# Four gate tiles of a hybrid layer as 2x2x2 block products with seven multiplications

## The chip, the cores and the metric

The kernel runs on one core of a Trainium2 chip. The core has a matrix engine (TensorE, PE in the profile, with its weight loads as PEld), a vector engine (VectorE, DVE), a scalar engine (ScalarE, ACT), a general one (GpSimd, POOL), and queues that issue transfers from memory; SP is the one that issues most. Each engine takes its instructions in the order of the program and waits at semaphores for the others. The metric is the device time of one execution in microseconds (us); the median of three runs is taken.

## The reference

One layer on x of 512 tokens by 1024 channels, in fp32, with 8 attention heads, a memory of 256 tokens and an FFN with 2816 hidden channels:

```python
h = rms_norm(x, norm_mix)
q_a, k_a, v_a, u_b, gate_b, gate_c, g_a, g_b = split(h @ w_in)   # 6 x 512, then 2 x 1024 columns
o_a = stick_breaking_attention(q_a, k_a, v_a)
y_b = gate_b * causal_depthwise_conv(gate_c * u_b, conv_w)
merged = sigmoid(g_a) * (o_a @ w_branch_a) + sigmoid(g_b) * (y_b @ w_branch_b)
x = x + merged @ w_mix_out
x = x + memory_cross_attention(rms_norm(x), rms_norm(mem), w_mem_q, w_mem_kv, w_mem_o)
gate, up = split(rms_norm(x, norm_ffn) @ w_ffn_in)
x = x + (silu(gate) * up) @ w_ffn_out
return rms_norm(x, norm_final)
```

The change is in g_a and g_b, the two gates of 1024 channels each, and in what lies beside them.

## The kernel before

Activations are kept transposed, as tiles of 128 channels by 512 tokens. To keep fp32's precision, each operand is split into a high part (rounded, on ACT) and a remainder (on DVE), and each product is made of three matmuls, high by high, high by remainder, remainder by high (`mm3`, lines 159 to 161). A weight tile of 128 x 1024 (512 KB) is loaded by SP into a buffer `wr`, of which there are four, cast on ACT to `wh` (line 154) and its remainder `wl` made on DVE (line 155).

A wide product of one column tile with 8 tiles of x is 24 matmuls of 512 columns. The layer has also the other kind: two column tiles, two halves of the tokens and two tiles of the inner dimension form a 2x2x2 block product, which is made with seven multiplications in place of eight (`product`, line 710; the products go to PSUM tiles z, v and y). It needs sums of blocks of x (`forms_of`, from two tiles xe and xo: c and d are the sums; high parts xf, xoh, xch, xdh, remainders xol, xcl, xdl) and of the weights (`ffn_raw` on DVE or POOL; `ffn_form` makes their high and low parts), and sums of the products behind it (`reads`, `second`). The seven products are 12 matmuls of 256 columns each, at a time. Memory queries and FFN are made so before; the gates are not.

Stages: projections and the attention, one step after another (`scores`: ACT makes Abs, Exp and Ln of z as e, DVE adds, POOL masks; `parts`: e is cast and split into l; `weights`: matmuls of l with negtri, line 437, then Exp as a, masked by POOL and split on DVE into ah and al; `values`). TensorE's order there is written out; projections, convolution and the first gate tiles fill its time between the steps, and weight loads go along with them. The orders of ACT, DVE, POOL and SP in this stage come out of a scheduler. Then a loop over the 8 column tiles of the gates: per tile two gate products (`pr`, 24 matmuls each; DVE multiplies by the tokens' norm factor; ACT takes the sigmoid), the two branch products (`br`, 12 matmuls each), two multiplications by DVE (line 583), their sum (line 584) and its split (`mh`, `ml`). Then the output projection, tile by tile (`r`), which adds x (`residual`, line 630) from tiles that SP loads into xpool, eight buffers, and makes the forms for the memory queries.

From the memory queries on, the orders of TensorE, ACT and DVE are written out. The SP queue takes its loads in one order, and a load whose buffer isn't free holds those behind it.

## Time and profile before

| | |
|---|---|
| median of 3 runs | 852.45 us (852.08 to 853.06) |
| the profiled execution | 852.67 us, of which 851.0 are the span |
| TensorE busy | 843.5 us (99%) |
| VectorE busy | 644.3 us (76%) |
| ScalarE busy | 460.9 us (54%) |
| GpSimd busy | 77.2 us (9%) |
| gates, tiles 4 to 7 | 236.60 to 301.90 us |
| output projection | 301.90 to 345.50 us |

The page gives each engine's busy time and share, the clock that the throttle granted TensorE, and the chain that ended last. Since matmuls follow one another with hardly a gap, the list of what TensorE waited for is the view to look at when something is added, and the timeline, where it is queried by engine and stretch, shows how near each chain came. Rows of the timeline read: start, length, engine, line, operation, outputs<-inputs, shape, count; idle time of the engine just before and what ended it in brackets.

### The profile page before, as it was taken

How to read it: one execution, taken by the hardware profiler on the slowest of the kernel's cores; microseconds unless marked ns; L12 is line 12 of the kernel's file. 1: busy time of each engine (PE TensorE's matmuls, PEld its weight loads, DVE VectorE, ACT ScalarE, POOL GpSimd, SP SyncE). 2: the span in 40 equal slices, each digit the busy share in tenths (PEclk: the TensorE clock that was granted, in tenths of full speed). 3: DMA queues.
4: the chain of work that ended last, by engine and by line, in shares of the span. 5: the costliest groups of instructions: out<-in, count | busy, mean ns of one | idle time of the engine just before them, and what ended most of it. 6: DMA issues, size and time to landing. Idle time of an engine off the chain costs nothing.

```text
span 851.0 us, 13532 instructions
## 1 busy us (share of the span) xinstructions
PE 843.5 (99%) x5200; PEld 757.9 (89%) x5200; DVE 644.3 (76%) x1106; ACT 460.9 (54%) x822; POOL 77.2 (9%) x101
## 2 busy tenths in 40 slices
PE   9999999999999999999999999999999999999997
PEld 7878787888888888999988889999999999888997
DVE  8769889987444467878765889888888778876864
ACT  7566767665333245665654666555445556552444
POOL 1011112211000001000000110111111110010002
PEclk9999999999999999999999999999999999999999
DMA  8332332318333334655331427777677775362312
GB/s 298 130 118 76 99 101 73 101 51 271 112 99 99 99 99 113 158 188 189 124 109 65 137 60 199 182 187 178 175 189 186 191 188 170 128 149 68 97 38 100
DMA packets 47217, 114.71 MB, mean 135 GB/s; under 512 B 4912, under 2 KB 9008, under 8 KB 47152
## 3 DMA queue, kind: packets, MB, share of 16 engines
q1 hardware_dynamic: 38704, 97.82, 35.1%
q0 software_dynamic: 8160, 15.73, 11.7%
q8 instruction: 41, 0.67, 0.3%
q14 instruction: 24, 0.20, 0.1%
q10 hardware_dynamic: 288, 0.29, 0.1%
HBM read 110.65 MB, written 2.10 MB: 132 GB/s over the span
## 4 chain that ended last, share of the span: by engine, by line
PE 99%; DVE 0%; POOL 0%; issue 0%; DVEq 0%; ACT 0%; POOLq 0%
PE z L710 20%; PE y L710 10%; PE pr L159 8%; PE pr L161 8%; PE pr L160 8%; PE v L710 5%; PE r L159 3%; PE r L161 3%; PE r L160 3%; PE f L160 3%; PE f L161 3%; PE f L159 3%; PE v L265 3%; PE br L159 2%; PE br L161 2%; PE br L160 2%
## 5 line engine op out<-in xcount | busy, mean ns | idle before, releaser
L154 ACT CAST wh<-wr 128x1024 fp32r<-128x1024 f32 x90 | 94.2, 1050 | 130.0 <-issue 48.1
L155 DVE TENSOR_TENSOR wl<-wr,wh 128x1024 fp32r<-128x1024 f32 x90 | 109.6, 1221 | 18.0 <-ACT wh L154 17.2
L159 PE MATMUL pr<-xgh,wh 128*128 128x512 f32 x288 | 112.6, 391 | 0.0
L160 PE MATMUL pr<-xgl,wh 128*128 128x512 f32 x288 | 112.3, 390 | 0.0
L161 PE MATMUL pr<-xgh,wl 128*128 128x512 f32 x288 | 112.2, 390 | 0.0
L710 PE MATMUL z<-xdh,wf 128*128 128x256 f32 x480 | 95.7, 283 | 0.0
L710 PEld LDWEIGHTS z<-xdh,wf 128*128 128x128 f32 x480 | 78.9, 192 | 0.0
L710 PE MATMUL z<-xdl,wf 128*128 128x256 f32 x240 | 67.9, 283 | 0.0
L733 ACT COPY sa<-z 128x256 f32<-128x256 f32 x52 | 19.4, 373 | 85.5 <-PE z L710 85.4
L161 PEld LDWEIGHTS pr<-xgh,wl 128*128 128x128 f32 x288 | 54.0, 188 | 11.4
L159 PEld LDWEIGHTS pr<-xgh,wh 128*128 128x128 f32 x288 | 54.1, 188 | 11.2 <-DVE rv L128 0.3
L160 PEld LDWEIGHTS pr<-xgl,wh 128*128 128x128 f32 x288 | 54.1, 188 | 10.9
L701 DVE TENSOR_TENSOR wf<-s,wf 128x512 fp32r<-128x512 f32 x60 | 41.3, 690 | 22.8 <-ACT wf L700 21.6
L667 POOL DMA_DIRECT2D ws<-in_w_ffn_in_dram x22 | 26.4, 1202 | 301.8 <-DMA ws<-in_w_ffn_in_dram 140.4
L700 ACT CAST wf<-ws 128x512 fp32r<-128x512 f32 x60 | 36.9, 618 | 24.9 <-PE r L160 10.0
L159 PE MATMUL f<-acth,wh 128*128 128x512 f32 (+1 forms) x144 | 49.3, 342 | 0.0
L160 PE MATMUL f<-actl,wh 128*128 128x512 f32 (+1 forms) x144 | 49.3, 342 | 0.0
L161 PE MATMUL f<-acth,wl 128*128 128x512 f32 (+1 forms) x144 | 49.1, 342 | 0.0
L692 DVE TENSOR_TENSOR wf<-wg,wf 128x1024 fp32r<-128x1024 f32 x30 | 36.7, 1224 | 16.0 <-ACT wf L691 15.9
L710 PE MATMUL y<-xch,wf 128*128 128x256 f32 x240 | 48.5, 283 | 0.0
L710 PE MATMUL v<-xoh,wf 128*128 128x256 f32 x240 | 48.5, 283 | 0.0
L710 PE MATMUL z<-xf,wf 128*128 128x256 f32 x360 | 48.4, 283 | 0.0
(295 smaller groups left out, 2296.0 us busy)
## 6 DMA issues: line engine op xcount, KB each, us to landing
wr<-in_w_in_dram SPq DMA_DIRECT2D x36, 512.0 KB, 3.5
ws<-in_w_ffn_in_dram SPq DMA_DIRECT2D x22, 512.0 KB, 3.9
ws<-in_w_ffn_in_dram POOLq DMA_DIRECT2D x22, 512.0 KB, 6.0
wg<-in_w_ffn_in_dram SPq DMA_DIRECT2D x22, 512.0 KB, 4.8
wr<-in_w_ffn_out_dram SPq DMA_DIRECT2D x14, 512.0 KB, 3.5
a<-in_w_ffn_in_dram SPq DMA_DIRECT2D x22, 256.0 KB, 4.9
wr<-in_w_branch_dram SPq DMA_DIRECT2D x8, 512.0 KB, 3.5
wr<-in_w_mix_out_dram SPq DMA_DIRECT2D x8, 512.0 KB, 3.4
```

What stands on the lines that cost most here:

```text
L154: after(nc.scalar.copy(h2, raw), lead[-1:])
L155: lows.append(nc.vector.tensor_tensor(out=l2, in0=raw, in1=f(h2), op=ALU.subtract))
L159: nc.tensor.matmul(ps, a[0], b[0], start=start, stop=False, **kw)
L160: nc.tensor.matmul(ps, a[0], b[1], start=False, stop=False, **kw)
L161: nc.tensor.matmul(ps, a[1], b[0], start=False, stop=stop, **kw)
L265: nc.tensor.matmul(vps[t], xg[k][a][:, sl], wv[k][b], start=k == 0 and (a, b) == (0, 0), stop=k == KD - 1 and a == 1)
L667: nc.gpsimd.dma_start(s13, a[:, 0:4:3, :], accum_op=ALU.add)
L692: nc.vector.tensor_tensor(out=lo, in0=pair, in1=f(hi), op=ALU.subtract)
L700: nc.scalar.copy(hi, raw)
L701: nc.vector.tensor_tensor(out=lo, in0=raw, in1=f(hi), op=ALU.subtract)
L710: nc.tensor.matmul(ps[:, :HS], a, b, start=i < 3 and k == 0 and j == 0, stop=k == KP - 1 and j == 2, skip_group_check=True)
L733: nc.scalar.copy((s[:, :HS], None, None, s[:, HS:], t[:, :HS], t[:, :HS])[i], z)
```

## The change

The gates of the last four column tiles (4 to 7) are made as 2x2x2 block products with seven multiplications: the two column tiles of a block are gate A's and gate B's of the same channels, and per tile there are 84 matmuls of 256 columns in place of 48 of 512. Their weights come as a new input in block order, and are loaded and summed like those of the FFN, four forms ahead (`GATE_AHEAD`). The sums of x that they need are made of x times the norm's gains: `pair_load` loads two tiles of x once more into a buffer `wr` in the loop over the first four tiles (on SP), `pair_forms` scales them on ACT (lines 774 to 776), makes the sums on DVE and splits them on both; the high parts and remainders of x itself are there from the attention's projections. The order of TensorE, ACT and DVE in these four tiles is written out: product, sums of products (`gate_reads`, `gate_second`), next forms, and behind each tile's last product its branch products. The splits of the merged tiles are made later: tiles 0 to 3 during the last tile's products, 4 to 7 behind the last branch; until then the merged sums stay in xpool. The x of the residual, for which xpool's eight buffers served before, is now taken from the unit pool (`f(unit("x"))`), and the split parts of d (xdh, xdl) from xpool (`new=spare`).

```diff
+GATES = 4
+GM = QM + D // (2 * P)
+GATE_AHEAD = 4
...
-    def split(src, s, scale=None, cols=512):
-
-        hi, lo = unit(s + "h", cols), unit(s + "l", cols)
+    def split(src, s, scale=None, cols=512, new=unit):
+
+        hi, lo = new(s + "h", cols), new(s + "l", cols)
...
+    def spare(s, cols=512):
+        return xpool.tile([P, cols], F32R, tag="x", name=nm(s), padded_shape=[P, S])
...
-    merged = []
-    for m in range(KD):
-        sig = []
-        for j in range(2):
-            if (m, j) not in gates:
-                gate(m, j)
-            t = gates.pop((m, j))
-            sigmoid = nc.scalar.activation(t, t, AF.Sigmoid)
-            after(sigmoid, exps[-2:])
-            sig.append(t)
-        w = load_w(wbr_d[m])
-        for j, act in ((1, yb), (0, oT)):
-            ps = mmtile("br")
-            gemm(ps, w, act, 4 * j)
-            nc.vector.tensor_tensor(out=sig[j], in0=ps, in1=sig[j], op=ALU.mult)
-        nc.vector.tensor_tensor(out=sig[0], in0=sig[0], in1=sig[1], op=ALU.add)
-        merged.append(split(sig[0], "m"))
...
+        return c, d
+
+    def forms_of(xe, xo):
+
+        b11 = xe[:, :HS]
+        c, d = sums_of(xe, xo)
...
-        (oh, ol), (ch, cl), (dh, dl) = split(xo, "xo"), split(c, "xc"), split(d, "xd")
+        (oh, ol), (ch, cl), (dh, dl) = split(xo, "xo"), split(c, "xc"), split(d, "xd", new=spare)
+        return listed((u[:, :HS], u[:, HS:]), oh, ol, ch, cl, dh, dl)
+
+    def listed(first, oh, ol, ch, cl, dh, dl):
         a, b = slice(0, HS), slice(HS, S)
-        return [(u[:, a], u[:, b]), (oh[:, a], ol[:, a]), (ch[:, a], cl[:, a]),
-                (dh[:, a], dl[:, a]), (ch[:, b], cl[:, b]), (dh[:, b], dl[:, b]),
-                (oh[:, b], ol[:, b])]
+        return [first, (oh[:, a], ol[:, a]), (ch[:, a], cl[:, a]), (dh[:, a], dl[:, a]),
+                (ch[:, b], cl[:, b]), (dh[:, b], dl[:, b]), (oh[:, b], ol[:, b])]
...
-                xm = xpool.tile([P, S], F32, tag="x", name=nm("x"))
+                xm = f(unit("x"))
...
-        src = wfi_d[m] if m < NF else wfp_d[m - NF] if m < QM else wmq_d[m - QM]
+        src = (wfi_d[m] if m < NF else wfp_d[m - NF] if m < QM else wmq_d[m - QM] if m < GM
+               else wga_d[m - GM])
...
-            xh, xl = (x2f if m < NF else af if m < QM else x1f)[k][i]
+            xh, xl = (x2f if m < NF else af if m < QM else x1f if m < GM else x0f)[k][i]
...
+    merged, halves0, raw_m = [], [], []
+
+    def branch(m, sig, w):
+        for j, a in ((1, yb), (0, oT)):
+            ps = mmtile("br")
+            gemm(ps, w, a, 4 * j)
+            nc.vector.tensor_tensor(out=sig[j], in0=ps, in1=sig[j], op=ALU.mult)
+        t = f(spare("m"))
+        nc.vector.tensor_tensor(out=t, in0=sig[0], in1=sig[1], op=ALU.add)
+        raw_m.append(t)
+
+    def squash(t):
+        sigmoid = nc.scalar.activation(t, t, AF.Sigmoid)
+        after(sigmoid, exps[-2:])
+        return sigmoid
+
+    def pair_load(k2):
+        xp = wpool.tile([P, 2, S], F32, tag="wr", name=nm("xp"))
+        nc.sync.dma_start(xp, xT_d[2 * k2 * P:(2 * k2 + 2) * P, :].rearrange("(j p) t -> p j t",
+                                                                            p=P))
+        return xp
+
+    def pair_forms(k2, xp):
+        for j in range(2):
+            k = 2 * k2 + j
+            nc.scalar.activation(xp[:, j, :], xp[:, j, :], AF.Copy, scale=g_mix[:, k:k + 1])
+        c, d = sums_of(xp[:, 0, :], xp[:, 1, :])
+        (eh, el), (oh, ol) = xg[2 * k2:2 * k2 + 2]
+        return listed((eh[:, :HS], el[:, :HS]), oh, ol, *split(c, "xc"), *split(d, "xd"))
+
+    x0f = []
+    for m in range(KD - GATES):
+        sig = []
+        for j in range(2):
+            if (m, j) not in gates:
+                gate(m, j)
+            sig.append(gates.pop((m, j)))
+            squash(sig[j])
+        if m < KD // 2:
+            xp = pair_load(m)
+        branch(m, sig, load_w(wbr_d[m]))
+        if m < KD // 2:
+            x0f.append(pair_forms(m, xp))
+
+    def gate_reads(m, i):
+        b = banks[m]
+        z, g, t = b["z"][:, :HS], b["g"] if "g" in b else None, b["t"]
+        lo, hi = slice(0, HS), slice(HS, S)
+        if i == 0:
+            b["z0"] = tmp("fg")
+            nc.scalar.copy(b["z0"][:, lo], z)
+        elif i == 1:
+            b["g"] = g = b["z0"]
+            nc.vector.tensor_tensor(out=g[:, lo], in0=b["v"][:, :HS], in1=g[:, lo], op=ALU.add)
+        elif i == 3:
+            nc.scalar.copy(g[:, hi], z)
+        elif i == 4:
+            nc.scalar.copy(t[:, hi], z)
+        elif i == 5:
+            for u, half in ((z, lo), (t[:, hi], hi)):
+                nc.vector.scalar_tensor_tensor(out=t[:, half], in0=u, scalar=-1.0,
+                                               in1=r0b[:, half], op0=ALU.mult, op1=ALU.mult)
+            squash(t)
+        elif i == 6:
+            nc.vector.tensor_tensor(out=g[:, hi], in0=b["y"][:, :HS], in1=g[:, hi], op=ALU.add)
+            nc.vector.tensor_tensor(out=g, in0=g, in1=r0b, op=ALU.mult)
+            b["sigmoid"] = squash(g)
+
+    def gate_second(m):
+        b = banks[m]
+        t = b["t"][:, HS:]
+        nc.vector.tensor_tensor(out=t, in0=b["y"][:, :HS], in1=t, op=ALU.add)
+
+    gs = order(GM, GATES)
+    for n in range(GATE_AHEAD + SUM_AHEAD):
+        ffn_raw(*gs[n], nc.gpsimd)
+    for n in range(GATE_AHEAD):
+        ffn_form(*gs[n])
+    with tc.manual_schedule(engines={mybir.EngineType.PE, mybir.EngineType.Activation,
+                                     mybir.EngineType.DVE}):
+        wb, last_m = {}, GM + GATES - 1
+        for n, (m, i) in enumerate(gs):
+            product(bank_of(m, i), m, i)
+            if i == 1 and m > GM:
+                gate_second(m - 1)
+            elif (m, i) == (last_m, 5):
+                gate_second(m)
+            gate_reads(m, i)
+            if n + GATE_AHEAD < len(gs):
+                ffn_form(*gs[n + GATE_AHEAD])
+            if n + GATE_AHEAD + SUM_AHEAD < len(gs):
+                ffn_raw(*gs[n + GATE_AHEAD + SUM_AHEAD])
+            if i == 3:
+                wb[m] = load_w(wbr_d[KD - GATES + m - GM])
+            if i == 6:
+                b = banks.pop(m)
+                branch(KD - GATES + m - GM, (b["g"], b["t"]), wb[m])
+                sigmoid = b["sigmoid"]
+            if m == last_m and i in (1, 2, 3, 4):
+                merged.append(split(raw_m[len(merged)], "m"))
+        while len(merged) < KD:
+            merged.append(split(raw_m[len(merged)], "m"))
...
+    def by_block(w, n=None):
+
+        w = w.reshape(-1, 2, P, NB, 2, P) if n is None else (
+            w.reshape(-1, 2, P, 2, n, P).transpose(0, 1, 2, 4, 3, 5))
+        return w.transpose(3, 2, 4, 1, 0, 5).reshape(-1, P, 2048)
...
+        "w_gates": by_block(w_in[0][:, O_A:O_A + 2 * D], KD)[KD - GATES:],
```

The orders of the engines change in three places that are looked at below. In the ACT order of a late attention step (e is the step's z through Abs, Exp and Ln; a the Exp of the step before), before:

```order
L154 CAST wh_1880<-wr_1878 128x1024
L400 ACTIVATE e_1648<-z_1644 128x256
L445 ACTIVATE a_1659<-z_1511 128x512
L445 ACTIVATE a_1661<-z_1512 128x512
L401 ACTIVATE e_1648<-e_1648 128x256
L402 ACTIVATE e_1648<-e_1648 128x256
L410 COPY carry_397<-z_1644 1x256
L373 CAST l_1673<-e_1648 128x256
L154 CAST wh_1997<-wr_1995 128x1024
```

and after (line numbers are 3 higher there):

```order
L157 CAST wh_1880<-wr_1878 128x1024
L776 ACTIVATE xp_2106<-xp_2106,gcol 128x512 x2
L403 ACTIVATE e_1648<-z_1644 128x256
L448 ACTIVATE a_1659<-z_1511 128x512
L448 ACTIVATE a_1661<-z_1512 128x512
L404 ACTIVATE e_1648<-e_1648 128x256
L405 ACTIVATE e_1648<-e_1648 128x256
L413 COPY carry_397<-z_1644 1x256
L376 CAST l_1673<-e_1648 128x256
L157 CAST wh_1997<-wr_1995 128x1024
```

The two scalings of the first x pair, xp, now stand between a weight cast and the Abs. At the end of the gates, DVE before (g is a gate, br a branch product, x the residual):

```order
L583 TENSOR_TENSOR g_2753<-br_2762,g_2753 128x512
L583 TENSOR_TENSOR g_2719<-br_2776,g_2719 128x512
L584 TENSOR_TENSOR g_2719<-g_2719,g_2753 128x512
L155 TENSOR_TENSOR wl_2935<-wr_2932,wh_2934 128x1024
L174 TENSOR_TENSOR ml_2792<-g_2719,mh_2791 128x512
L630 TENSOR_TENSOR x_2827<-r_2802,x_2827 128x512
```

and after, where fg and sb are a tile's two gates (A and B) and y the PSUM tile of its last product:

```order
L757 TENSOR_TENSOR sb_2696<-br_3018,sb_2696 128x512
L757 TENSOR_TENSOR fg_2709<-br_3032,fg_2709 128x512
L759 TENSOR_TENSOR m_3046<-fg_2709,sb_2696 128x512
L822 TENSOR_TENSOR sb_2862<-y_2920,sb_2862 128x256
L811 SCALAR_TENSOR_TENSOR sb_2862<-z_2861,r0b_338 128x256
L811 SCALAR_TENSOR_TENSOR sb_2862<-sb_2862,r0b_338 128x256
L158 TENSOR_TENSOR wl_3167<-wr_3164,wh_3166 128x1024
L815 TENSOR_TENSOR fg_2875<-y_2920,fg_2875 128x256
L158 TENSOR_TENSOR wl_3227<-wr_3224,wh_3226 128x1024
L816 TENSOR_TENSOR fg_2875<-fg_2875,r0b_338 128x512
L757 TENSOR_TENSOR sb_2862<-br_3079,sb_2862 128x512
L757 TENSOR_TENSOR fg_2875<-br_3093,fg_2875 128x512
```

The first reading of the last tile's y (line 822) stands behind the branch multiplications and the sum of the tile before; weight remainders stand among them, and the splits `ml` of tiles 4 to 7 come after the last sum. In the forms of the last pair of x tiles ahead of the memory queries, DVE before:

```order
L603 TENSOR_TENSOR xf_3172<-xr_3125,xf_3172 128x256
L174 TENSOR_TENSOR xol_3176<-xr_3164,xoh_3175 128x512
L174 TENSOR_TENSOR xcl_3180<-c_3166,xch_3179 128x512
L174 TENSOR_TENSOR xdl_3184<-c_3167,xdh_3183 128x512
L735 TENSOR_TENSOR qa_3238<-v_3237,sa_3226 128x256
```

and after:

```order
L596 TENSOR_TENSOR xf_3503<-xr_3456,xf_3503 128x256
L177 TENSOR_TENSOR xol_3507<-xr_3495,xoh_3506 128x512
L177 TENSOR_TENSOR xdl_3515<-c_3498,xdh_3514 128x512
L177 TENSOR_TENSOR xcl_3511<-c_3497,xch_3510 128x512
L732 TENSOR_TENSOR qa_3569<-v_3568,sa_3557 128x256
```

The remainder of d stands ahead of that of c; the high parts on ACT have changed places in the same way, and so have both ahead of the FFN.

13 lines of the change are left out of this document (6 added, 7 removed).

## The prediction

> **What bounds the kernel now.** I read the page first, then the waits of TensorE, then windows and stretches of the timeline where the change puts something. Two parts of the page:
>
> ```profile
> span 851.0 us, 13532 instructions
> PE 843.5 (99%) x5200; PEld 757.9 (89%) x5200; DVE 644.3 (76%) x1106; ACT 460.9 (54%) x822; POOL 77.2 (9%) x101
> PEclk9999999999999999999999999999999999999999
> PE 99%; DVE 0%; POOL 0%; issue 0%; DVEq 0%; ACT 0%; POOLq 0%
> ```
>
> And the whole answer on what TensorE (PE) waited for:
>
> ```profile
> engine line waited for: us in total, times, longest us
> PE warm L224 <- DVE neg L91: 1.6, 1, 1.6
> ```
>
> So TensorE is the path from end to end, at full granted clock: work taken off it shortens the run by as much, and every new wait of it lengthens the run by as much. The profiled execution took 852.67 us, of which 851.0 is the span; the median of the three runs is 852.45, 0.2 below. About 0.2%, 1.7 us, is what a measurement of this kernel can tell from no change: under 850.75 is faster, over 854.15 slower.
>
> **The gain.** Windows of the gate stage before (tiles 4 to 7) and of a stretch of the FFN that already consists of such products (length; busy time and instructions of PE, PEld, DVE, ACT, POOL; granted clock; share of the DMA engines; GB/s):
>
> ```profile
> 236.60:301.90 65.30, 65.30 (x290) 54.07 (x289) 30.59 (x36) 20.67 (x26) 0.00 (x0) 1.00 0.30 97
> 506.89:567.09 60.20, 60.20 (x503) 60.11 (x502) 54.09 (x96) 34.30 (x63) 7.22 (x6) 1.00 0.74 178
> ```
>
> Before, four tiles are 4 x 72 = 288 matmuls of 512 columns, 65.3 / 288 = 0.2267 us each. A 256-column one takes 60.2 / 503 = 0.120 us: more than half of 0.2267, with weight loading (PEld) busy for all of the window. Per tile 48 x 0.2267 = 10.88 us of gate matmuls become 7 x 12 x 0.120 = 10.08; 0.80 saved, four times: 3.2 us. The branch matmuls stay.
>
> [...]
>
> VectorE (DVE) has room: the FFN window needs 54.09 / 60.2 x 10.08 = 9.1 us of it per tile. A gate tile needs about as much, plus a branch's share (two multiplications and a sum of 0.69, a weight remainder of 1.22: 3.3), in 10.08 + 5.44 = 15.5 us. The sums, splits and scalings of x go into the attention, where nothing of them is on TensorE: their work is covered, and what counts is who waits behind them (waits 1 to 3).
>
> **Wait 1: x at the head of ScalarE (ACT).** In the order of ACT the two scalings of the first x pair stand in front of the Abs of a late attention step. Its chain before:
>
> ```profile
> wr<-in_w_branch_dram SPq DMA_DIRECT2D x2, 512.0 KB, 3.5
> 154.37 0.33 SPq L147 DMA_DIRECT2D wr<-in_w_branch_dram  x1
> 155.39 0.38 ACT L400 ACTIVATE e<-z 128x256 f32<-128x256 f32 x1
> 155.66 1.08 ACT L445 ACTIVATE a<-z 128x512 f32<-128x512 f32 x2
> 156.32 1.89 POOL L359 TENSOR_SCALAR_AFFINE_SELECT a<-a 128x128 f32<-128x128 f32 x2 [6.92 <-ACT a L445]
> 157.07 0.42 ACT L402 ACTIVATE e<-e 128x256 f32<-128x256 f32 x1
> 158.75 0.42 DVE L453 CAST ah<-a 128x512 fp32r<-128x512 f32 x1
> 159.75 0.42 DVE L403 SCALAR_TENSOR_TENSOR e<-z,e 128x256 f32<-128x256 f32 x1
> 160.21 0.36 ACT L410 COPY carry<-z 1x256 f32<-1x256 f32 x1 [2.71 <-DVE e L403]
> 160.24 1.13 POOL L359 TENSOR_SCALAR_AFFINE_SELECT e<-e 128x256 f32<-128x256 f32 x1 [2.04 <-DVE e L403]
> 161.41 0.41 ACT L373 CAST l<-e 128x256 fp32r<-128x256 f32 x1 [0.84 <-POOL e L359]
> 161.85 0.42 DVE L374 TENSOR_TENSOR l<-e,l 128x256 fp32r<-128x256 f32 x1 [0.74 <-ACT l L373]
> 162.61 0.40 PE L437 MATMUL z<-l,negtri 128*128 128x256 f32 x2
> 346.31 0.73 ACT L633 ACTIVATE xr<-x,gcol 128x512 f32<-128x512 f32 x1 [0.33 <-DVE x L630]
> 346.94 0.62 ACT L642 ACTIVATE sq<-x 128x512 f32<-128x512 f32 x1
> ```
>
> The x load takes the queue slot of the branch weight, which is issued at 154.37 and needs 3.5: it lands at 157.9. Two scalings follow, 0.63 from start to start (346.31 to 346.94), so the Abs starts at 159.2 in place of 155.39, 3.85 late. POOL's mask of a then starts at 160.2, its first half ends at 161.1, and DVE, which in its order takes ah and a convolution step (0.6) ahead of e, reaches e at 162.2 in place of 159.75: it had 2.26 in hand (157.49 to 159.75), and uses part of it. From there the distances stay: 162.7 POOL, 163.9 ACT, 164.3 DVE, which ends at 164.7; TensorE follows 0.25 later at 164.95 in place of 162.6. That is 2.3 us. All of TensorE is queued behind it, so nothing covers it. Ends: 1.5, if all of the 2.26 absorbs; 3.7, if none does. I take 2.3, since the DVE order gives that point.
>
> That a row of ACT holds what is written behind it is seen at 160.21: ACT stood 2.71 us for DVE and none of its later rows ran. [...]
>
> **Wait 2: the second x pair.** It stands on ACT before a weight cast and the next step's Abs; its second scaling and one weight cast stand ahead of the two casts l, and on DVE g and wl come ahead of the two remainders l:
>
> ```profile
> 176.52 0.93 ACT L373 CAST l<-e 128x384 fp32r<-128x384 f32 x2 [0.94 <-DVE e L424]
> 177.07 1.03 DVE L374 TENSOR_TENSOR l<-e,l 128x384 fp32r<-128x384 f32 x2 [0.30 <-ACT l L373]
> 178.01 0.69 DVE L311 TENSOR_TENSOR g<-pr,r0b 128x512 f32<-128x512 f32 x1
> 178.61 1.22 DVE L155 TENSOR_TENSOR wl<-wr,wh 128x1024 fp32r<-128x1024 f32 x1
> 180.56 0.97 PE L437 MATMUL z<-l,negtri 128*128 128x384 f32 x4
> ```
>
> Now ACT is free at 175.6 for the scaling (0.63) and the cast (1.04), so wl can't start before 177.3; if g comes where it did, at 178.0, wl ends at 179.8, the remainders (0.52 each) at 180.8, and TensorE goes on at 181.05 in place of 180.56: 0.5. Ends: 0, if g is ready earlier and wl follows the cast at once (remainders done at 179.7); 1.1, if g, wl, scaling and cast all add up (0.60 + 1.14 + 0.63 + 0.95 + 0.25 to TensorE, less the 2.46 between 178.10 and 180.56). I take 0.5, the value that the rows give.
>
> **Wait 3: end of attention.** The third x load goes ahead of branch weights, whose cast came just in time:
>
> ```profile
> 193.59 0.33 SPq L147 DMA_DIRECT2D wr<-in_w_branch_dram  x1
> 197.57 1.05 ACT L154 CAST wh<-wr 128x1024 fp32r<-128x1024 f32 x1 [1.59 <-PE pr L160]
> 201.43 0.69 DVE L583 TENSOR_TENSOR g<-br,g 128x512 f32<-128x512 f32 x1 [0.22 <-PE br L161]
> ```
>
> The cast begins 3.98 after the issue, and TensorE's first use of the sublayer's output follows within a few us. Before, that load had 256 KB pieces of x around it; now it has 512 KB of x just ahead on SP's queue, and ACT has two scalings to fit in. The cast may come from 0 to 1.0 later (a weight cast of 1.05 ahead of it at most); I take 0.3, nearer to the low end, because ACT stood idle 1.59 before it.
>
> **Wait 4: last two gate tiles.** The last tile's final product writes a PSUM tile that DVE must have read; that read stands behind both branch multiplications and the sum of the tile before. The same instructions before:
>
> ```profile
> 301.64 0.39 PE L161 MATMUL br<-oh,wl 128*128 128x512 f32 x1
> 302.07 0.69 DVE L583 TENSOR_TENSOR g<-br,g 128x512 f32<-128x512 f32 x1 [1.96 <-PE br L161]
> 302.79 0.69 DVE L584 TENSOR_TENSOR g<-g,g 128x512 f32<-128x512 f32 x1
> L743 DVE TENSOR_TENSOR sb<-y,sb 128x256 f32<-128x256 f32 x22 | 9.2, 418 | 0.0
> ```
>
> From the branch's last matmul (its slot ends at 301.87) to the multiplication 0.2, then 0.72, 0.61, 0.42, and 0.25 to TensorE: 2.2 us, of which one product (12 x 0.120 = 1.44) covers part: 0.75, taken as 0.7. Ends 0.4 and 1.2 (a weight remainder of 1.22 slipping in between, less what it hides). The merged splits 4 to 7 behind the last branch: the sum ends at 303.5, then four remainders and a wl at 0.6 and 1.14, so the one for tile 5 ends at 305.8 and TensorE wants it at 301.87 + 18 x 0.2267 = 305.95, less than 0.25 later: 0.1. The residual's x, loaded ahead before, is now issued on SP behind the last mix weight that waits for tile 3's remainder (about 305.6 by the row of DVE that it waits for):
>
> ```profile
> x<-in_xT_dram SPq DMA_DIRECT2D x8, 256.0 KB, 5.6
> ```
>
> It lands by 311.2, and the PSUM buffer that it holds up is wanted two blocks of 24 matmuls after the stage's start, at 301.9 + 10.9 = 312.8, less 0.7 for the addition: nothing, with 0.9 in hand. Ends of these: 0 and 0.3 for the splits; the x, if it comes a landing later, is part of the much slower rival.
>
> **Wait 5: the swap of two remainders.** In the forms of the last pair, at the start of the memory queries and again of the FFN, DVE now makes xdl before xcl. Both places before:
>
> ```profile
> 349.68 0.69 DVE L174 TENSOR_TENSOR xcl<-c,xch 128x512 fp32r<-128x512 f32 x1
> 350.42 0.39 PE L710 MATMUL y<-xcl,wf 128*128 128x256 f32 x1
> 505.65 0.68 DVE L174 TENSOR_TENSOR xcl<-c,xch 128x512 fp32r<-128x512 f32 x1
> 506.39 0.39 PE L710 MATMUL y<-xcl,wf 128*128 128x256 f32 x1
> ```
>
> TensorE takes xcl 0.05 after it is ready, so it is the wait already; 0.6 later (one remainder, start to start) costs 0.6 at each place, 1.2. The later xdl products want xdl only after that. Ends 0.6 (one place) and 1.4.
>
> **The sum.** -3.2 + 2.3 + 0.5 + 0.3 + 0.7 + 0.1 + 1.2 = +1.9: 854.6 against 852.67 of the profiled execution, and 854.4 against the median. With all low ends (1.5, 0, 0, 0.4, 0, 0.6) it is -0.7: 851.8; with all high ends (3.7, 1.1, 1.0, 1.2, 0.3, 1.4) it is +5.5: 858.0, both against the median.
>
> **The rivals.**
> - Faster: the attention absorbs the x loads, in that x lands sooner or DVE's 2.26 us in hand and later slack take all of it. With waits 1 to 3 gone, wait 4 at 0.4 and one of the two swaps, it is -3.2 + 0.4 + 0.6 = -2.2, 850.3. It stops being faster where wait 1 passes 0.5. For it speak that slack and ACT's share of 54%; against it the row at 160.21, and that the load's shortest way (3.5 in both loads of that window) is what I used. Chance 0.16.
> - No change: wait 1 at its low end, waits 2 and 3 small: -3.2 + 1.5 + 0.2 + 0.2 + 0.6 + 1.2 = +0.5, 853.0 (852.95 against the median). For it is that each of these has a zero end. Chance 0.31.
> - A full gain: the gate products come at half of a wide matmul, 0.2267 / 2 = 0.1133, since their weights are loaded with less beside them than in the FFN window. Then a tile saves 10.88 - 9.52 = 1.36, the stage 5.4, and the sum is -0.3: 852.2, no change. The 60.11 of weight loading in 60.20 speaks against it. Chance 0.03. [...]
> - Much slower: the gate tiles' weights come late. Their loads (three of 512 KB and one of 256 KB a tile, one of them an adding load issued by POOL) are new in a stretch that moved 97 GB/s; a load that is late by one landing, 3.5, with a form's share of it hidden, holds ACT and then TensorE for some 2.5 us: 856.9. Against it: the FFN does this at 178 GB/s, in 10.1 us a tile and not 15.5. Chance 0.12.
>
> **How the numbers follow.** The forecast, with its terms near their values, has 0.38, and goes from 854.2 to 856. With the much slower rival, slower has 0.50; no change 0.31 + 0.03 = 0.34; faster 0.16. The low end leaves out less than half of the faster cases and reaches to 850.4; the high one takes in late weights: 857.6.
>
> **What would show it.** Right: TensorE's list of waits, now one row, has the matmul with negtri (line 440 in the changed kernel) behind DVE l with about 2.3 us, a product in the gates behind the read of y with 0.7, y behind xcl twice with 0.6; a window over the last four gate tiles of 62 us plus that wait; the first scaling on ACT with an idle of 2 to 3 us ahead, ended by the load of x. Wrong: x landing before ACT gets there, matmuls of the gates that are not 0.120 apart, or a wait of TensorE on a weight cast inside the gate tiles.

## The result, and the profile after

The changed kernel takes 858.77 us (median of 6 runs, 856.74 to 859.29), the kernel before on the same chip 852.61 (6 runs, 851.97 to 853.06): a ratio of 1.007, with an interval of 1.0057 to 1.0083. It is slower by 6.2 us. The forecast was slower too, but by 1.9, and the time lies above its range.

The profiled execution took 858.25 us, with a span of 856.4. Page of the changed kernel, the lines that answer to those shown of before:

```profile
span 856.4 us, 13976 instructions
PE 843.1 (98%) x5344; PEld 762.5 (89%) x5344; DVE 671.3 (78%) x1169; ACT 479.9 (56%) x866; POOL 81.5 (10%) x106
PE 90%; DVE 4%; issue 2%; DMA 2%; ACT 1%; POOL 0%; SPq 0%; DVEq 0%; POOLq 0%
```

TensorE's busy time fell by only 0.4 us, and it is no longer the whole of the chain that ended last: DVE, DMA and ACT have shares. What TensorE waited for, one row before, seven now (us in total, times, longest):

```profile
PE r L162 <- DVE x L625: 1.7, 1, 1.7
PE warm L227 <- DVE neg L94: 1.6, 1, 1.6
PE y L706 <- DVE xcl L177: 1.2, 2, 0.6
PE z L706 <- DVE xf L596: 0.9, 1, 0.9
PE z L440 <- ACT l L376: 0.6, 1, 0.6
PE z L706 <- ACT xf L595: 0.6, 1, 0.6
PE y L706 <- DVE sb L822: 0.5, 1, 0.5
```

The last product of attention (line 440), the reading of y by sb and the two waits for xcl had been forecast. The rows for r and for xf had not. A wait costs some 0.16 more than its row says, since the matmul ahead of it is modelled as 0.39 long in a slot of 0.227 (0.28 in one of 0.120).

To see where the time went I read the start of each stage off TensorE's timeline. Before: the first product of gate tile 4, the first matmul of the output projection, of the memory queries, and of the memory's scores behind them:

```profile
236.59 0.39 PE L159 MATMUL pr<-xgh,wh 128*128 128x512 f32 x1
...
301.87 0.39 PE L159 MATMUL r<-mh,wh 128*128 128x512 f32 x1
...
345.39 0.88 PE L710 MATMUL z<-xf,wf 128*128 128x256 f32 x6
...
384.60 0.28 PE L159 MATMUL km<-mgh,wh 128*128 128x256 f32 x1
```

The same four after:

```profile
238.37 0.28 PE L706 MATMUL z<-xgh,wf 128*128 128x256 f32 x1
...
301.27 0.39 PE L162 MATMUL r<-mh,wh 128*128 128x512 f32 x1
...
346.99 1.24 PE L706 MATMUL z<-xf,wf 128*128 128x256 f32 x9
...
390.42 0.28 PE L162 MATMUL km<-mgh,wh 128*128 128x256 f32 x1
```

The differences of these starts give a ledger:

| stage | before | after | difference |
|---|---|---|---|
| up to gate tile 4 | 236.59 | 238.37 | +1.8 (0.25 of it ahead of attention) |
| gate tiles 4 to 7 | 65.28 | 62.90 | -2.4 |
| output projection | 43.52 | 45.72 | +2.2 |
| memory queries | 39.21 | 43.43 | +4.2 |
| the rest of 5.4 | | | -0.4 |

The gates did what they were to do. The loss stands in the two stages behind them, which the prediction had priced at 0 and 0.6. The rest is the second swap (+0.6) against an FFN that is 1.0 shorter (last section).

Two things are seen in these stages. The first is the timeline of the output projection in the changed kernel, SP's queue at its start, and two x that came late (the third, and the fifth, the first for which TensorE had to wait; start, length, instruction, idle time before it):

```profile
304.72 0.33 SPq L150 DMA_DIRECT2D wr<-in_w_mix_out_dram  x1
305.10 0.42 SPq L622 DMA_DIRECT2D x<-in_xT_dram  x1
309.66 0.38 SPq L658 DMA_DIRECT2D ws<-in_w_mem_q_dram  x1
310.09 0.46 SPq L622 DMA_DIRECT2D x<-in_xT_dram  x1
...
322.27 0.69 DVE L625 TENSOR_TENSOR x<-r,x 128x512 f32<-128x512 f32 x1 [0.66 <-DMA x<-in_xT_dram]
...
335.15 0.69 DVE L625 TENSOR_TENSOR x<-r,x 128x512 f32<-128x512 f32 x1 [1.41 <-DMA x<-in_xT_dram]
335.99 0.47 PE L162 MATMUL r<-mh,wh 128*128 128x512 f32 x1 [1.73 <-DVE x L625]
```

From the second to the fifth, each x is issued behind a weight of the memory queries, and that weight waits for a buffer; the last three follow the fifth at once (327.71). The list of SP's waits in this stage names who frees it:

```profile
SPq L660 <- DVE wl L158: 10.3, 2, 5.5
SPq L658 <- DVE wl L158: 8.1, 2, 4.0
```

The wl behind the fourth x starts on DVE at 320.39, behind the forms of the first pair; the one behind the fifth at 325.21, behind the addition of the third x, which had itself waited 0.66 for its load. So it is a ring: x, what DVE makes of it, a wl, a weight load, a later x. A load that starts late comes out late a few rounds on: DVE waits 0.40 for the second x, 0.66 for the third, and at 335.15, with the fifth, 1.41. There TensorE, whose PSUM buffer DVE should have emptied, waits 1.73.

The second is the clock at the start of the memory queries. Windows of the changed kernel (length; busy time of PE, PEld, DVE, ACT, POOL; granted clock; DMA share; GB/s):

```profile
350.00:354.00 4.00, 2.56 (x17) 1.92 (x15) 3.54 (x9) 3.48 (x8) 0.00 (x0) 1.00 0.81 233
354.00:358.00 4.00, 3.42 (x17) 3.16 (x16) 3.42 (x7) 1.03 (x2) 1.20 (x1) 0.65 0.60 145
358.00:362.00 4.00, 4.00 (x33) 4.00 (x32) 1.50 (x3) 3.13 (x7) 0.00 (x0) 0.92 0.98 237
```

The three waits for xf, xf and xcl lie in the first window and at the start of the second; then the granted clock falls to 0.65 and 0.92, where it was 1.00 in every such window before, up to the last matmul. In windows of 0.2 us it is 0.50 from 355.2 to 358.6 and full on both sides: half speed for 3.4 us. The clock alone lost (0.35 + 0.08) x 4 = 1.7 us, the waits 2.1 and three times 0.16: 4.3, which is the stage's 4.2.

Ahead of the half clock TensorE had only short waits close together, the longest of 0.9 (more of this in the last section).

### The profile page after: what moved, and what is told of

Same layout as the page of the kernel before. It is cut to its first block, busy times and chain, and to the rows that moved or that the text cites. A ratio compares the mean times of both kernels' runs of the same rounds, so it can differ in the third digit from the quotient of the medians.

```text
span 856.4 us, 13976 instructions
## 1 busy us (share of the span) xinstructions
PE 843.1 (98%) x5344; PEld 762.5 (89%) x5344; DVE 671.3 (78%) x1169; ACT 479.9 (56%) x866; POOL 81.5 (10%) x106
## 4 chain that ended last, share of the span: by engine, by line
PE 90%; DVE 4%; issue 2%; DMA 2%; ACT 1%; POOL 0%; SPq 0%; DVEq 0%; POOLq 0%
PE z L706 22%; PE y L706 11%; PE v L706 5%; PE pr L162 5%; PE pr L164 5%; PE pr L163 5%; PE f L162 3%; PE f L163 3%; PE f L164 3%; PE v L268 3%; PE r L162 3%; PE r L163 3%; PE r L164 2%; PE br L163 2%; PE br L162 2%; PE br L164 2%
## 5 line engine op out<-in xcount | busy, mean ns | idle before, releaser
L706 PE MATMUL z<-xdh,wf 128*128 128x256 f32 x544 | 108.8, 284 | 0.0
L162 PE MATMUL pr<-xgh,wh 128*128 128x512 f32 x224 | 87.7, 391 | 0.0
L163 PE MATMUL pr<-xgl,wh 128*128 128x512 f32 x224 | 87.4, 390 | 0.0
L164 PE MATMUL pr<-xgh,wl 128*128 128x512 f32 x224 | 87.3, 390 | 0.0
L697 DVE TENSOR_TENSOR wf<-ws,wf 128x512 fp32r<-128x512 f32 x68 | 46.9, 690 | 10.8 <-ACT wf L696 10.7
L706 PE MATMUL z<-xch,wf 128*128 128x256 f32 x272 | 54.5, 283 | 0.0
L706 PEld LDWEIGHTS z<-xdl,wf 128*128 128x128 f32 x272 | 52.0, 191 | 0.2
L696 ACT CAST wf<-s 128x512 fp32r<-128x512 f32 x68 | 42.3, 622 | 15.5 <-DVE s L674 14.8
L164 PEld LDWEIGHTS pr<-xgh,wl 128*128 128x128 f32 x224 | 42.0, 188 | 8.8
L162 PEld LDWEIGHTS pr<-xgh,wh 128*128 128x128 f32 x224 | 42.1, 188 | 8.6 <-DVE rv L131 0.3
```

What stands on the lines that cost most here:

```text
L162: nc.tensor.matmul(ps, a[0], b[0], start=start, stop=False, **kw)
L163: nc.tensor.matmul(ps, a[0], b[1], start=False, stop=False, **kw)
L164: nc.tensor.matmul(ps, a[1], b[0], start=False, stop=stop, **kw)
L696: nc.scalar.copy(hi, raw)
L697: nc.vector.tensor_tensor(out=lo, in0=raw, in1=f(hi), op=ALU.subtract)
L706: nc.tensor.matmul(ps[:, :HS], a, b, start=i < 3 and k == 0 and j == 0, stop=k == KP - 1 and j == 2, skip_group_check=True)
```

## The experiments

The theory to begin with: the loss behind the gates comes from where x and the parts of d are kept. In the unit pool, x can be loaded only when a tile of the attention or the gates comes free; in xpool before, it was loaded ahead. The rival: it comes from what the gate tiles now leave for later (four merged splits, weight forms, the written-out order), whatever the pool.

**The pool undone.** x of the residual from xpool again, the split parts of d from the unit pool again; all else as changed.

```diff
-        (oh, ol), (ch, cl), (dh, dl) = split(xo, "xo"), split(c, "xc"), split(d, "xd", new=spare)
+        (oh, ol), (ch, cl), (dh, dl) = split(xo, "xo"), split(c, "xc"), split(d, "xd")
...
-                xm = f(unit("x"))
+                xm = xpool.tile([P, S], F32, tag="x", name=nm("x"))
```

> x of the residual again in xpool (its eight buffers, now shared with the merged sums) and the split parts of d in the unit pool; in the order of SP seven of the eight x loads then stand ahead of the last mix weight, and on ACT the scaling of x stands ahead of the cast of a weight form again. Theory A (the late load of x makes the output projection wait 1.9 us, and what is late there makes the start of the memory queries wait 2 us more and lose some 1.7 us to a lower clock): both go, and with them the swap of the two remainders at both places; about 6 us faster than the changed kernel, 852 to 853. Rival B (the lag comes from the splits of tiles 4 to 7 and from weight forms on DVE behind the gates, not from x): the projection's wait and the memory queries' wait stay, only the swap goes, 0.6 twice: about 857.5.

Measured: 852.84 us (852.09 to 854.0, 10 runs), a ratio of 1.0003 to the kernel before (0.9994 to 1.0012). That is 5.9 below the changed kernel. What TensorE waits for in it, beside the row of before:

```profile
PE z L440 <- ACT l L376: 0.5, 1, 0.5
PE y L706 <- DVE sb L822: 0.5, 1, 0.5
PE br L162 <- ACT oh L176: 0.5, 1, 0.5
PE br L163 <- DVE ol L177: 0.2, 1, 0.2
```

And SP's queue at the end of its gates and in the output projection:

```profile
298.32 8.29 SPq L622 DMA_DIRECT2D x<-in_xT_dram  x7
```

Seven of the eight x are issued one after another, ahead of the memory queries' weights. The ring is open: no wait for x, xf or xcl, and no dip of the clock (mean 0.999). The theory holds as far as this: without the pool change, the loss behind the gates is gone. It doesn't yet say that the pool change alone makes it. The x of the residual and the parts of d were only ever moved together, so their shares aren't told apart.

**The swap undone alone.** Only the order of the splits, by two order constraints (`parted` holds each split's cast and remainder, `after` puts the first behind the second); pools as changed.

```diff
+        for i in range(2):
+            after(parted[-1][i], [parted[-2][i]])
```

> Only an order is added: the high part and the remainder of d come behind those of c, as before the change. Theory (my price of the swap, 0.6 at each of two places): 1.2 us faster than the changed kernel, 857.5, with the wait for xcl gone twice. If the lower clock at the start of the memory queries hangs on the sum of the waits there (2.0 us, now 1.4), its 1.7 us go too: 856. If it hangs on the waits for xf, it stays.

Measured: 855.86 us (855.75 to 856.81, 4 runs), 1.004 (1.0025 to 1.0054), 2.9 below the changed kernel. The two waits for xcl are gone, which is 1.2, as in the prediction. The wait of r for x is gone as well (1.7 in its row). In this profile, then, the splits' order acts on the ring too, which I had not thought of: the wl that stood behind the forms of the first pair now starts at 319.48, ahead of their last two remainders, and the fourth and fifth x are issued at 321.16 and 326.29 in place of 322.08 and 327.71. The waits for xf stay, the first longer than it was (1.3 for 0.6), and so does the dip (0.57 at 352 to 356). So the time is that of the forecast with a full clock, 856, but it came about in another way:

```profile
PE z L709 <- ACT xf L596: 1.3, 1, 1.3
PE z L709 <- DVE xf L597: 0.9, 1, 0.9
```

**The pool change alone, on the kernel before.** No product of the gates touched.

```diff
-        (oh, ol), (ch, cl), (dh, dl) = split(xo, "xo"), split(c, "xc"), split(d, "xd")
+        (oh, ol), (ch, cl), (dh, dl) = split(xo, "xo"), split(c, "xc"), split(d, "xd", new=spare)
...
-                xm = xpool.tile([P, S], F32, tag="x", name=nm("x"))
+                xm = f(unit("x"))
```

> One part of the change alone, on the kernel before: the residual's x from the unit pool and d's split parts from xpool; the gates stay wide products, and the merged tiles are split as before. On SP the x loads then stand behind the mix weights and between the memory queries' weights, and the swap of the two remainders is there. Theory A (this part alone makes the loss behind the gates): the swap's 1.2, plus waits for x in the output projection and at the memory queries, and some lower clock: 856 to 858.5. Rival B (late splits and gate products are needed for it): only the swap, 853.8.

Measured: 853.91 us (853.05 to 854.68, 10 runs), 1.0017 (1.0008 to 1.0026): 1.7 above the kernel before, not 6. TensorE's waits in it:

```profile
PE y L713 <- DVE xcl L174: 1.2, 2, 0.6
PE z L713 <- DVE xf L606: 0.6, 1, 0.6
PE r L159 <- DVE x L633: 0.2, 1, 0.2
```

The two xcl are there, but r waits 0.2 and one xf is missing, and the clock doesn't dip (mean 0.999). The total is the rival's, 853.8, but not its account, which was the swap alone. Its first two x are issued at 299.70 and 305.56, after the change at 305.10 and 310.09: one round earlier in the ring. The sum agrees: 2.0 of waits, four times 0.16, less the 1.0 that the FFN gains by the placing of d (last section) are 1.6. So neither theory is right alone. The pool change by itself costs 1.7 and the rest of the change 0.3 (the pool undone, against 852.59 on its chip); together they cost 6.2. The pool change closes the ring, and behind the gate tiles the ring starts one round later. That the splits on DVE make it late is argued, not shown: in the changed kernel the mix weight ahead of the first x (304.72) waits for a wl that DVE makes from 303.47, behind the last sum and a split, but no run moves the splits by themselves.

**One cast on ACT behind a scaling.** At the start of the memory queries the changed kernel's ACT has, in its timeline:

```profile
346.97 0.62 ACT L696 CAST wf<-ws 128x512 fp32r<-128x512 f32 x1 [3.35 <-PE r L163]
347.49 0.72 ACT L628 ACTIVATE xr<-x,gcol 128x512 f32<-128x512 f32 x1
...
350.09 0.72 ACT L628 ACTIVATE xr<-x,gcol 128x512 f32<-128x512 f32 x1 [1.36 <-DVE x L625]
```

A weight cast stood 3.35 us for TensorE, while the scaling behind it could have run: DVE had added the seventh x from 344.96 to 345.64. The eighth scaling comes at 350.09, before the change at 346.31. The edit puts the cast behind the seventh scaling:

```diff
+        cast = nc.scalar.copy(hi, raw)
+        if (m, i) == (QM, 4):
+            after(cast, scaled[6:7])
```

> Only an order is added to the changed kernel: on ACT the cast of the last weight form ahead of the memory queries comes behind the scaling of the seventh x tile, as before the change. x is late and the remainders are swapped as in the changed kernel. Theory A' (the cast waits for a buffer that the last r matmuls free, and holds the scaling; it makes the waits for xf, 1.7 with their latencies, and so the lower clock behind them, 1.7): 855.0 to 855.5, the waits for xf gone and the clock at 1.00. Rival (the seventh x tile is late anyway because its addition is): 858 to 859, waits for xf as they were.

Measured: 856.38 us (854.79 to 858.0, 4 runs), 1.0047 (1.0029 to 1.0065), 2.4 below the changed kernel. Its list has one xf left, with 0.6 in place of 0.9 and 0.6, and its clock stays full in the window that had 0.65:

```profile
354.00:358.00 4.00, 4.00 (x34) 3.90 (x34) 3.54 (x7) 1.72 (x5) 1.20 (x1) 1.00 0.81 223
```

In this execution, then, 0.9 of waits and the 1.7 of the clock came from one instruction's place on ACT. The median lies between the two forecasts, and the dip isn't gone from every run: the four have mean clocks of 1.0 (854.79 us), 0.998 (855.93, the profiled one), 0.996 (856.83) and 0.997 (858.0), and among the other kernels a mean under 0.998 is seen only in those whose profile has a dip.

**The x pairs without load and scaling.** The sums for the gates are made from what is there already: high part plus remainder, two additions on DVE per pair; no load, nothing on ACT.

```diff
     def pair_forms(k2, xp):
-        for j in range(2):
-            k = 2 * k2 + j
-            nc.scalar.activation(xp[:, j, :], xp[:, j, :], AF.Copy, scale=g_mix[:, k:k + 1])
-        c, d = sums_of(xp[:, 0, :], xp[:, 1, :])
         (eh, el), (oh, ol) = xg[2 * k2:2 * k2 + 2]
+        xe, xo = tmp("xe"), tmp("xo")
+        nc.vector.tensor_tensor(out=xe, in0=f(eh), in1=f(el), op=ALU.add)
+        nc.vector.tensor_tensor(out=xo, in0=f(oh), in1=f(ol), op=ALU.add)
+        c, d = sums_of(xe, xo)
```

> The pairs of x are neither loaded nor scaled again: DVE adds the high part and the remainder of the scaled x that the projections already use (two additions of 0.69 us a pair); nothing of them on SP or ACT. Theory (the head of ACT's queue in the attention costs what TensorE loses there, 2.1 us from the first late matmul with negtri to the gates): about 2 us faster than the changed kernel, 856.7, and TensorE's wait for ACT's l gone. Rival (it is the sums and splits on DVE and ACT that come late, and DVE now has more): no faster, 858.5 to 859.5, with waits of TensorE in the attention.

Measured: 858.34 us (857.92 to 858.39, 4 runs), 1.0065 (1.005 to 1.008): no nearer than the changed kernel. Yet the attention gave the whole cost back. From the norm's product at its head to the first product of gate tile 4 it takes 208.9 us, as before the change, and the waits at lines 440 and of br are gone. The time went again in the output projection:

```profile
323.82 0.47 PE L162 MATMUL r<-mh,wh 128*128 128x512 f32 x1 [1.93 <-DVE x L625]
...
324.00:328.00 4.00, 4.00 (x12) 3.13 (x12) 2.78 (x4) 2.11 (x4) 1.28 (x2) 0.60 0.54 98
```

Here the wait for x is followed by a clock of 0.60, and the clock falls once more in the memory queries, at 355.5. In the changed kernel r waited 1.7 and the clock stayed at 1.00. So the 1.5 us that the attention gave back were eaten by a second dip (1.7) and 0.2 more of waiting: with the ring closed behind it, an edit can gain in its own stage and show nothing in the total.

**The last tile's reading of y moved ahead of the branch multiplications.**

```diff
-            elif (m, i) == (last_m, 5):
-                gate_second(m)
             gate_reads(m, i)
+            if (m, i) == (last_m, 4):
+                gate_second(m)
```

> The last tile's first reading of y is written before the branch multiplications of the tile ahead of it. Theory (wait 4 is that reading standing behind them): TensorE's wait for it, 0.5 in the list, goes: 0.6 us faster than the changed kernel, 858.2. Rival (DVE is late there anyway): the wait only moves to another reading, same time.

Measured: 858.27 us (854.54 to 859.23, 5 runs), 1.0051 (1.0032 to 1.0071); the total can't be told from the changed kernel's, and that it meets the forecast of 858.2 says little with such a spread. The profile says more: the wait for sb is gone, and the four gate tiles take 62.16 us (239.50 to 301.66) in place of 62.90, 0.74 less. The r behind it waits 2.0 in place of 1.7.

**The three together.** Pool undone, pairs from their parts, reading of y moved.

> Three of the edits together, on the changed kernel: x of the residual in xpool again (and d's parts in the unit pool), x pairs of the gates from the high part and the remainder without a load or a scaling, and the last reading of y ahead of the branch multiplications. Theory (the gates gain 3.1 us, and what ate it are the heads of ACT and SP in the attention, 2.4, wait 4, 0.7, and the late x): nothing is left of the waits, 3.1 us faster than the kernel before, 849.5. Rival (DVE's two additions a pair, and its load in the gates, put other waits in their place): 851 to 853.

Measured: 849.65 us (849.38 to 850.1, 5 runs), 0.9968 (0.9956 to 0.9981), and of TensorE's waits only the one of before is left:

```profile
PE warm L227 <- DVE neg L94: 1.6, 1, 1.6
```

This is faster than both kernels. Its gates take 62.16 us in place of 65.28, 3.1 less, and the span is 847.8 in place of 851.0, 3.2 less. With every new wait gone, the product's gain comes out as it was priced.

**More tiles.** The same with five and with six of the eight gate tiles as block products (GATES = 5, 6; the pairs' sums divided among the remaining wide tiles), and with six and the sums made in the attention's steps 13 to 16.

```diff
-GATES = 4
+GATES = 5
...
+        for k2 in range(m * (KD // 2) // (KD - GATES), (m + 1) * (KD // 2) // (KD - GATES)):
+            x0f.append(pair_forms(k2, None))
```

> The same with five gate tiles as block products. If the gain is matmul time alone, each tile is worth 0.80: 848.7. If the sums of x for it come too late in the attention or the weights are late, no faster than with four, 849.5 to 851.

> The same with six gate tiles (all but the two that fill the attention). If the gain is matmul time alone, 1.6 more than with four: 847.9. If the sums or the weights come too late at the start of the gates, 849 to 852, with TensorE waiting at the first products.

> As the three edits together, with six gate tiles, and the pairs of x summed and split during the last three steps of the attention and not behind them. If the waits of the six-tile kernel at the start of the gates came from late sums: 848, with TensorE waiting for nothing there. If DVE has no room for them in the attention: 852 or more, with waits of TensorE in its last steps.

Measured: 857.22 us with five (856.64 to 857.91, 4 runs; 1.0057, 1.0043 to 1.007), 863.18 with six (862.64 to 864.07, 4 runs; 1.0124, 1.0109 to 1.014), 863.61 with six and sums in the attention (862.75 to 865.26, 4 runs; 1.0132, 1.0117 to 1.0147). The largest wait of each, in this order:

```profile
PE pr L162 <- DVE rv L131: 3.8, 1, 3.8
```
```profile
PE y L706 <- ACT xch L176: 3.9, 2, 2.1
```
```profile
PE var L195 <- DVE g L314: 4.2, 1, 4.2
```

With five and with six the times lie far above both forecasts; the third is a case of its rival, 852 or more with waits in the attention's last steps. In the first and third DVE is late within the attention, in the second ACT and DVE at the first product. I read this as sums and splits of x that, with fewer wide tiles left in front, no longer lie beside work that has room for them; no run separates that from other causes. Each is followed by a dip of the clock (0.71 and 0.87 at 188 to 196 us with five; 0.88, 0.50 and 0.77 at 216 to 228 with six; 0.81, 0.50 and 0.84 at 180 to 192 in the third). By the price above more blocks would save 0.8 each; the waits and the clock cost several times that.

**The clock by itself.** The kernel of the three edits, with two and with four idle operations on DVE (a maximum of c with itself, which changes nothing) in the forms of the last pair ahead of the memory queries. So waits come where the changed kernel had them, and the rest of the program is the same.

```diff
+        for _ in range(again):
+            nc.vector.tensor_tensor(out=c, in0=c, in1=c, op=ALU.max)
```

> As the three edits together (849.65), and the maximum of c with itself taken twice (two more DVE instructions of 0.69 us, the value stays) in the forms of the last pair of x tiles ahead of the memory queries: xcl comes 1.2 us later, where TensorE waits for it. If a wait costs its own length alone: 850.8 to 851.1 and the clock stays at 1.00. If a wait of this length makes the clock go down, 1.7 us more: 852.6.

> The same with four of them; the high part then also starts only behind the last, so xcl comes 2.4 to 3.2 us later. If a wait costs its own length alone: 852.0 to 852.9, clock 1.00. If a wait that is long enough makes the clock go down to half for some 3.4 us: 853.8 to 854.6, with a window behind the wait that shows it.

Measured: with two 851.22 us (850.84 to 852.01, 10 runs; 0.9985, 0.9976 to 0.9995), with four 854.67 (854.24 to 855.14, 9 runs; 1.0026, 1.0016 to 1.0036): 1.6 and 5.0 above the kernel without them. With two, TensorE's list has three new waits of 0.6, 0.3 and 0.2. With four there is one more:

```profile
PE y L708 <- ACT xch L176: 1.5, 1, 1.5
```

The stretch behind them with two, and the two stretches with four:

```profile
350.00:354.00 4.00, 4.00 (x35) 4.00 (x35) 3.92 (x7) 2.50 (x6) 1.20 (x1) 1.00 0.53 127
```
```profile
350.00:354.00 4.00, 3.23 (x18) 3.03 (x19) 3.59 (x7) 1.22 (x4) 1.20 (x1) 0.78 0.62 161
354.00:358.00 4.00, 4.00 (x29) 4.00 (x28) 1.83 (x3) 2.67 (x6) 0.00 (x0) 0.79 0.96 241
```

Two: 1.1 of waits and three times 0.16 are 1.6, all of the cost, at full clock. Four: 2.6 of waits and four times 0.16 are 3.2, and the clock (0.22 + 0.21) x 4 = 1.7 more: 4.9 of the 5.0. So the clock's part of the changed kernel's loss is reproduced with no product, pool or load changed.

## Why the prediction was wrong in size

The direction was right. What failed is one term that the sum had at nothing, the late x of the residual, with what follows from it at the memory queries; the other terms held, or were too large.

**Gain: right.** Forecast 3.2; the four tiles took 62.16 us where nothing waits in them, 3.1 less. The rival of a full gain (5.4) is excluded.

**Waits 1 to 3: of the right kind, sum 3.1 forecast, 1.5 to 2.6 measured.** In the changed kernel the way to gate tile 4 grew by 1.8, 0.25 of which lies ahead of the attention. Its chain, as in the prediction:

```profile
158.33 1.33 ACT L776 ACTIVATE xp<-xp,gcol 128x512 f32<-128x512 f32 x2 [2.60 <-DMA xp<-in_xT_dram]
...
160.49 0.29 POOL L362 TENSOR_SCALAR_AFFINE_SELECT a<-a 128x128 f32<-128x128 f32 x1 [10.90 <-ACT a L448]
...
162.34 0.80 POOL L362 TENSOR_SCALAR_AFFINE_SELECT e<-e 128x256 f32<-128x256 f32 x1 [0.94 <-DVE e L406]
...
163.62 0.85 PE L440 MATMUL z<-l,negtri 128*128 128x256 f32 x2 [0.62 <-ACT l L376]
```

ACT stood 2.60 for the load, as forecast, and all behind it came late. TensorE waits at the matmul with negtri, but 0.6 for ACT's l, where 2.3 behind DVE's was forecast; with 0.16 as above, and a second matmul that starts 0.46 behind the first in place of 0.12, wait 1 is 1.1. The mask of a took 0.29 and that of e 0.80, where the rows of before had 1.89 for two and 1.13: the distances I carried over from before didn't hold, and why POOL was quicker here isn't shown. Nor is the 0.25 that the sum has between DVE's end and TensorE, an estimate: DVE's l ended at 164.04, and the weight load that took it began at 164.08. Wait 2 (0.5) has no row at all. Wait 3 (0.3) is 0.2 here. In the profile of the kernel with the pool undone the attention lost 2.4, and wait 3 more: the cast of the branch weight stood 2.37 for its load and began at 200.44 (197.57 before), the split oh came behind it, and the rows of br have 0.5 and 0.2. That the whole of it comes from the load and the scalings is shown by the kernel that has neither: 0.

**Wait 4: right.** 0.7 forecast, 0.74 by the kernel that takes it away.

**Wait 5: right.** Two waits of 0.6 for xcl, gone when the order is put back.

**The residual's x, "nothing, with 0.9 in hand": this step failed.** It looked at the first x against its PSUM buffer, and there it was right: r didn't wait for that one. But seven x follow, and those up to the fifth are each held on SP by a weight load that waits for DVE, which waits in turn for an earlier x. With the fifth the lead was used up. x took longer to land as well (median 7.0 us, 5.6 before, 5.3 with the pool undone). That isn't explained by loads standing among those of the weights: they do so too with the swap undone (5.3) and with the pool change alone (4.5). In place of 0 the projection lost 2.2, of which the wait for x explains 1.9; 0.3 isn't attributed to a row.

**The start of the memory queries, priced at 0.6 for the swap alone, failed with it.** It lost 4.2: 1.5 of listed waits for xf, because the last two x are added late (344.96 and 349.37, before 340.64 and 345.59) and because a weight cast on ACT stands in front of a scaling, 0.6 for the swap, 0.16 three times, and 1.7 by a clock that I had taken to be full, as on the page of before.

**The rivals.** "Much slower" had the gate weights late; no wait on a weight cast appears in the gate tiles. Its total of 856.9 was nearer than the forecast, but by another mechanism: that is luck.

**The sum.** From the forecast's +1.9 to the 5.4 by which the span grew: attention -1.6 (1.5 for 3.1), the head of the kernel +0.25, gates 0 (-2.4 is what gain, wait 4 and splits came to), projection +2.2, memory queries +3.6 (4.2 less the swap's 0.6), FFN -1.0: 1.9 + 3.45 = 5.35.

## What to carry to other kernels

A buffer is a place in a queue: when a tile moves from a pool that was filled ahead to one that comes free as the work goes on, follow its load round the whole ring (queue, buffer, who frees it, what that waits for) over several steps, not only to its first use. On an engine that never waited before, short waits close together (2.1 us in the changed kernel, 2.6 with four idle operations) cost 1.7 us beside their own length, as the clock was halved behind them for 3.4 us; price them as a group. Where a kernel has one closed ring, an edit elsewhere can gain in its own stage and show nothing in the total, so read the stage, and open the ring first.

## What was not expected of the hardware

**The clock fell where 2.2 us or more were lost in one stretch of 3.4 us, not behind every long wait.** Waits of 1.1 us in a few us (two idle operations) and single ones of 1.7 and 2.0 (r, in the changed kernel and in that with the reading of y moved) left it at 1.00. Sums of 2.1 and 2.6 within about 5 us, and a single one of 1.9 (r, pairs from their parts), took it down, at a cost of 1.7.

The profiles kept here say more. They have nine dips: two with pairs from their parts, one each in the changed kernel, with the swap undone, with the reading of y moved, with five tiles, with four idle operations and in the two kernels of six tiles. All have one form: a clock of 0.50 for 3.41 us, or for twice that (six tiles). And they lie on a raster. In the changed kernel's trace the record of the clock begins, with 1.00, at 7.07 us; the 0.50 at 355.23 lasts 3.413 us and begins 102.0 such steps later, and the 0.50 at 853.58, behind the last matmul, 248.0 steps later. In the trace of before, which has no dip, the record begins at 6.54, and the 0.50 behind the last matmul comes at 849.63, 247.0 steps later. With pairs from their parts the two dips, at 324.8 and 355.5, are 9 steps apart. Of each stretch of this raster, 0.227 or 0.120 us go to every matmul of 512 or 256 columns in it (others in proportion); the rest is what TensorE lost there, an estimate from the starts of the matmuls:

| kernel | stretch of 3.41 us from | lost in it, us | clock behind it |
|---|---|---|---|
| changed kernel | 351.8 | 2.4 | 0.50 |
| four idle operations | 348.9 | 2.3 | 0.50 |
| pairs from their parts | 321.4 | 2.2 | 0.50 |
| reading of y moved | 335.1 | 1.9 | 1.00 |
| five tiles | 182.8 | 1.6 | 1.00 |
| changed kernel | 334.8 | 1.4 | 1.00 |

In all fourteen profiles, up to the stretch with the last matmul, each stretch ahead of a dip lost 2.2 or more, and no stretch with a full clock behind it lost more than 1.9. The end doesn't fit: in the kernel before, the stretch from 842.8, with small matmuls of 2 and 128 columns, lost 2.5 by this estimate, and the clock behind it was 1.00. The wait of 2.0 that did nothing lay across two stretches (0.3 of it in the earlier), the one of 1.9 in a single one. By these profiles, then, it matters where on the raster a group of waits falls. No run placed a wait on purpose to test this, and none shows what sets the raster's start (6.54 and 7.07 above). Why the clock stayed low for a second stretch with the sums in the attention, though only 0.5 was lost in the first, is open.

**256-column matmuls were slightly faster with their x in another pool.** A group of 36 products in the FFN, in the chain of before and then in that of after (start, length, count):

```profile
567.09 4.32 PE z L710 x36
```
```profile
563.23 4.29 PE z L706 x36
```

They took 0.1200 each, and take 0.1192 where xdh and xdl lie in xpool; over the whole FFN, from the norm's product ahead of it to the first matmul behind it, 200.8 us stand against 201.8. By the mean distance of the FFN's matmuls (0.1194 against 0.1200) it is so in every kernel here with that placing, also in the one that changes nothing but pools, and in none without it. Why is open. A kernel that has this placing without the late x wasn't run.

**Run-to-run spread.** The changed kernel varies over 2.6 us (856.74 to 859.29), that with the reading of y moved over 4.7 (854.54 to 859.23), that with the cast moved over 3.2; the others with the closed ring over 0.5 to 1.6, the kernel before over 1.1, and the three edits together over 0.7. One execution of each was profiled, but every run has its mean granted clock, in which a dip is 1.7 of 857 us, 0.002. With the reading of y moved, the two runs at 1.0 took 854.54 and 856.87 us, the three at 0.996 858.27 to 859.23: a dip that comes in some runs and not in others makes part of the spread. It isn't the whole, since the fastest and the slowest run of the changed kernel both have 0.998.
